# Two tokens instead of four interleaved in the one-hot tiles of the gate matrices

## The chip, the cores and the metric

The kernel runs on one core of one Trainium2 chip. The metric is the time of one execution on the device in microseconds (us); lower is better. TensorE multiplies matrices, VectorE (DVE in the profile) and ScalarE (ACT) do the elementwise work, and SyncE (SP) issues the loads of weights. SBUF is the memory on the chip that the engines read, PSUM the one into which TensorE writes.

## The reference, cut to what matters

A model of two blocks with two layers each runs over 256 tokens of width 1024. The change lies in the PEER layer of the first block, which runs twice (once a layer). Each of 8 heads of a token picks 16 of 128 x 128 experts by the sum of two scores, and the outputs are summed with a softmax over the 16 as the gate:

```python
def block(t):
    q = (t @ w_pq).reshape(T, PEER_HEADS, 2, PEER_HALF)
    s = jnp.einsum('thpk,hpnk->thpn', q, sub_keys)
    top_s, top_i = lax.top_k(s, PEER_TOPK)
    cand_s = top_s[:, :, 0, :, None] + top_s[:, :, 1, None, :]
    cand_i = top_i[:, :, 0, :, None] * N_KEYS + top_i[:, :, 1, None, :]
    best_s, best_pos = lax.top_k(cand_s.reshape(...), PEER_TOPK)
    experts = jnp.take_along_axis(cand_i.reshape(...), best_pos, axis=-1)
    gate = jax.nn.softmax(best_s, axis=-1)
    act = jax.nn.gelu(jnp.einsum('td,thkd->thk', t, expert_down[experts]))
    return jnp.einsum('thk,thkd->td', gate * act, expert_up[experts])
```

## The kernel before

The kernel doesn't gather experts. It computes the activation of every one of the 16384 experts for every token (the "down" loop), multiplies it with a gate that is zero nearly everywhere, and multiplies the result with the whole second table (the "up" loop). For a token the gates form a matrix of 128 x 128 (first index by second index): the product of a one-hot matrix of rows [128 pairs of head and place, 128] and a one-hot matrix of columns [128 pairs, 128] whose ones are replaced by the gates. The gate is held as two float16 parts, so each token takes two matmuls that add up in PSUM.

**The down loop.** `peer` (from line 932) runs 64 steps `jp` of two units. A unit is `mtile` (line 233): 24 matmuls of 256 columns in float32r (8 blocks times three products of high and low parts), on weights that `Stream` loads over SP and splits into two parts, the high one by ScalarE (line 95) and the low one by VectorE (line 100). Three pairs of tiles `whi`, `wlo` take turns, so the split runs about two units ahead. `gelu` (line 965) puts the activations of a step away, ScalarE alone or with a multiply on VectorE (line 975) for the tokens whose gates came first.

**The background.** `peer_select` (line 798) is a generator; `peer` takes steps of it between units by a budget: a unit adds 1400 (`BG`), each step subtracts the number that it yields. It first finds the experts, and after each block of 128 tokens transposes the four lists (first index, second index, low part and high part of the gate) so that the pairs lie on partitions, into the table `TT` (lines 886 to 889). Then it makes the gate matrices, four tokens (a group) at a time, 64 groups a layer; a group takes two steps of 800 (`GC`):

- line 924: `is_equal` of a counter `io4` with the first and second index, on VectorE: both one-hot matrices of four tokens, 1024 float16 a partition.
- lines 926 and 927: the group before the last is put away by `evac` (line 894): ScalarE writes the part of the activations that isn't there yet (line 901), VectorE multiplies into the part that is (line 904). The latter grows as the loop goes on.
- line 928: the one-hot columns times the two parts of the gate, one instruction of 1024 float16.
- lines 909 to 915: `gate_mm` of the group before, eight matmuls of 128 x 128 x 128 in float16 for four tokens.

The one-hot tiles lie in `w6`, two sets that take turns. In a set the four tokens are interleaved: `O` is [128 pairs, 3 kinds, 128 places, 4 tokens], and token t's matrix is read as `O[:, s, :, t]`, one element of 2 bytes in every 8 bytes, both as the weights and as the moving operand:

```python
self.mm(o, O[:, 0, :, t], O[:, 1, :, t], True, False)
self.mm(o, O[:, 0, :, t], O[:, 2, :, t], False, True)
```

All other operands of matmuls in the down loop are read element after element. The order of the instructions on each engine is that of the program.

Of the kernel before, what the change touches and what calls it, by code (L numbers as in the profile page):

```python
# [20 lines left out]
# columns of the per-channel vectors, [128, count] each  # L21
# [10 lines left out]
class Stream:  # L32
    """Loads run ahead in one queue, in the order of use; tiles of weights are split into two
    float32r parts a few units before they are needed."""
# [36 lines left out]
    def mark(self):  # L71
        """nothing behind this place is split before it is passed"""
        self.todo.append((None, None, None))
# [44 lines left out]
    def raw_due(self, ahead=0):  # L118
        """the next raw item was loaded in front of the tiles in use, or not far behind"""
        return self.raw_q and self.raw_q[0][2] < self.at + ahead  # L120


class Kern:
# [16 lines left out]
    def __init__(self, nc, tc, ctx, a, out):  # L140
# [22 lines left out]
        # parts that change to float32r where the experts come  # L163
# [24 lines left out]
    def reset(self, lo=20480):  # L188
        """scratch: parts of the arena that the loads leave alone"""
        self.scr_at = [[self.arena, lo, 25088 if self.late else 26624], [self.arena, 0, 4096]]  # L190
        if self.a3 is not None:
            self.scr_at.append([self.a3, 0, 6144])

    def second(self):
        """from here on other tiles of scratch serve, and the loads have eight places"""
        S = self.S
        self.late = True
        self.w6 = self.arena[:, 25088:].rearrange("p (a b) -> p a b", b=256)
        self.fr0 = self.rp.tile([128, 4096], F32R, name="fr0", tag="r0")
        self.fw6 = self.rp.tile([128, 1024], F32R, name="fw6", tag="w6")  # L200
        S.drop = self.r0s
        for s in self.r0s:
            if any(s is f for f in S.free):
                S.free.remove(s)
        self.reset()

    def rounded(self):
        """float32r tiles for the experts"""
        self.a3 = None
        self.fa3 = self.rp.tile([128, 6144], F32R, name="fa3", tag="a3")  # L210
# [22 lines left out]
    def mtile(self, o, h):  # L233
        """o[128 outputs, 256 tokens] from the next unit of weights and h (d on partitions)."""
        hi, lo = self.S.next()
        self.poll()
        for k in range(8):
            s = slice(k * 128, (k + 1) * 128)
            self.mm3(o, (hi[:, s], lo[:, s]), (h[0][:, k, :], h[1][:, k, :]), k == 0, k == 7)

    def mtile2(self, os, h, lead=None):
        """two tiles at once, as the blocks of h come"""
# [39 lines left out]
    def gemv(self, l, m, cb, pool=0):  # L282
        """columns m, m + 1 of layer l's modulation, from the next raw item, without their bias"""
# [32 lines left out]
    def sq_mm(self, sq, ss, col, cols=8):  # L316
        """column sums of sq [128, 256], tokens on partitions, into columns col, cols + col"""
        for tb in range(2):
            o = tb * cols + col
            self.mm(ss[:, o:o + 1], sq[:, tb * 128:(tb + 1) * 128], self.ones[:, 0:1], True, True)  # L320

    def sums(self):
        """opens the sums of squares of x, tokens on partitions"""
# [4 lines left out]
    def sum_mm(self, sq, ss, k):  # L328
        """adds block k's squares [128, 256]"""
# [11 lines left out]
    def warm(self, n):  # L341
        """keeps the tensor engine's clock up while it would wait"""
# [5 lines left out]
    def warm_root(self):  # L348
        """has the table of the square root loaded"""
        self.nc.scalar.activation(self.one, self.epst, AF.Sqrt)  # L350

    def root(self, parts, n, d):
        """1 / sqrt(mean + eps) for the sums over the last axis of parts [128, n, ...]"""
# [6 lines left out]
    def spread(self, r):  # L360
        """r: for both blocks of tokens a column -> [128, 256], the same on all partitions"""
# [5 lines left out]
    def rstd(self, ss, r=None):  # L367
        """for both blocks of tokens a column of 1 / rms"""
# [6 lines left out]
    def norm(self, r, g, sc, sh, keep=None):  # L375
        """hi, lo of x * rstd * g * (1 + sc) + sh"""
# [25 lines left out]
    def lead(self, cb):  # L402
        """the first norm, two blocks at a time as the columns of their scale and shift come"""
# [31 lines left out]
    def x_step(self, ps, k, g, ss):  # L435
        """block k of x and its squares, whose sums the caller takes later"""
# [5 lines left out]
    def out_open(self):  # L442
        """x += g * (w_out^T h) with the channels of h in any order: four banks stay open"""
# [4 lines left out]
    def out_step(self, h, k, g=None):  # L448
        """one block of 128 channels of h; with g it is the last"""
# [29 lines left out]
    def add_mixer1(self, l, ada, every):  # L479
        """ada: pairs of modulation columns, their loads between those of the weights"""  # L480
# [15 lines left out]
    def mixer1(self, l, h, g, lead=None):  # L496
# [7 lines left out]
        # q and k, channels on partitions; heads c and c + 4 share a tile  # L504
# [47 lines left out]
        # v and the gating half, tokens on partitions  # L552
# [10 lines left out]
        # normalised q, k  # L563
# [46 lines left out]
        # y holds the three branches: attention 0..3, convolution 4..5, gating 6..7  # L610
# [79 lines left out]
        # group norm of the gating half  # L690
# [62 lines left out]
    def act(self, jp):  # L753
        """two activations of every token"""
# [3 lines left out]
    def up_order(self, i):  # L758
        """pairs whose room goes to the loads come first"""
# [3 lines left out]
    def add_peer_up(self, l, extra):  # L763
        """extra: modulation columns (layer, m0, n) whose loads go between"""
# [11 lines left out]
    def top16(self, src, n, val, idx, tmp):  # L776
        """top 16 of each row of src [128, cnt, n]; a generator, one step per row pair"""
# [19 lines left out]
    def peer_select(self, qT, keys, st):  # L797
        """top experts of every token and head -> gates and indices with the pairs on partitions,
        then the gate matrix of every token, multiplied into the activations."""
# [18 lines left out]
        TT = self.sm.tile([128, 4, 256], F16, name="TT")  # L818
# [12 lines left out]
        for tb in range(2):  # L831
# [16 lines left out]
            # softmax over the 16 best, in two float16 parts of gate * 2^15  # L848
# [10 lines left out]
            # place among the candidates -> places in the two lists  # L859
# [29 lines left out]
            nc.scalar.copy(TT[:, :, tb * 128:(tb + 1) * 128], pt)  # L889
            yield 10  # L890
        # gate matrices
# [18 lines left out]
        def gate_mm(O, t0):  # L910
            ps = self.bank()
            for t in range(4):
                o = ps[:, t * 128:(t + 1) * 128]
                self.mm(o, O[:, 0, :, t], O[:, 1, :, t], True, False)
                self.mm(o, O[:, 0, :, t], O[:, 2, :, t], False, True)
            pend.append((ps, t0))

        for t0 in range(0, 256, 4):
            # one-hot rows and columns, the columns times the gate's parts
            o = t0 // 4 % 2 * 3  # L920
            O = self.w6[:, o:o + 3, :].bitcast(F16).rearrange("p s (j t) -> p s j t", t=4)
            io = self.io4[:, None, :, :].to_broadcast([128, 2, 128, 4])
            bc = lambda i: TT[:, i:i + 2, None, t0:t0 + 4].to_broadcast([128, 2, 128, 4])
            TX(O[:, 0::2], io, bc(0), op=OP.is_equal)
# [3 lines left out]
            TX(O[:, 1:3], O[:, 2:3].to_broadcast([128, 2, 128, 4]), bc(2), op=OP.mult)  # L928
            if last is not None:
                gate_mm(*last)  # L930
            last = (O, t0)
# [6 lines left out]
    def peer(self, l, h, g2, extra):  # L938
# [16 lines left out]
        # the arena is the activations' from here on  # L955
# [40 lines left out]
        # up: tokens stationary, the table moving  # L996
# [76 lines left out]
    def gla(self, h, g):  # L1073
# [16 lines left out]
        # decay  # L1090
# [22 lines left out]
        # values, tokens on partitions  # L1113
# [52 lines left out]
        def states(hd):  # L1166
            """the state after every chunk"""
# [96 lines left out]
    def softplus(self):  # L1264
        """8 softplus(-lambda) and its negative"""
# [23 lines left out]
    def lru(self, h, g):  # L1289
# [28 lines left out]
        def wgate(w, o, bn, b):  # L1318
            """a gate of half b, block-diagonal"""
# [141 lines left out]
    def route(self, h, hf, ht):  # L1461
        """combine weights, one-hot groups and ranks of the tokens inside their group"""
# [10 lines left out]
        # the tokens, rows  # L1473
# [23 lines left out]
        # top two of each group of four  # L1497
# [9 lines left out]
        # the first group with the largest sum  # L1507
# [8 lines left out]
        # tokens of the same group in front of each token; their count after the last  # L1516
# [6 lines left out]
        # rank inside the group, ties to the lower index  # L1523
# [35 lines left out]
    def experts(self, S, base, ht, w, oh, rk, g2, r, first=None, lent=()):  # L1559
        """slots base..base+127 of every group through the group's four experts"""  # L1560
# [19 lines left out]
        def gather(g2_):  # L1580
            """the tokens of two groups"""
# [46 lines left out]
        def turn(e):  # L1628
            """the hidden rows of expert e, channels on partitions"""
# [97 lines left out]
    def moe(self, l, h, hf, g2):  # L1727
# [22 lines left out]
        # groups of more than 128 tokens: their other slots  # L1750
# [14 lines left out]
def build(nc, tc, ctx, a, out, upto=99):  # L1765
# [7 lines left out]
    # modulation columns that load while the experts' second table does  # L1773
    extra = [[(0, 40, 8, "c"), (1, 0, 48, "c"), (2, 0, 24, "c2")], [(2, 24, 24, "c2"), (3, 0, 48, "c2")]]

    # the order of every load of the program
# [76 lines left out]
def _mtiles(w):  # L1853
    """[1024, N] -> [N / 256, 128, 2 * 1024]: two tiles of 128 outputs to a load."""
# [5 lines left out]
def arrays_of(inputs):  # L1860
# [39 lines left out]
    # modulation, [4 layers, 24, 128, 2 * 1024]  # L1900
    ada = np.stack([f["w_ada"][0], f["w_ada"][1], f["ada_w_2"][0], f["ada_w_2"][1]])
    A["ada"] = c(ada.transpose(0, 2, 1).reshape(4, 24, 2, 128, 1024).transpose(0, 1, 3, 2, 4).reshape(4, 24, 128, 2048))
    # attention bias by distance
# [72 lines left out]
```

## Time and profile before

| | us |
|---|---|
| median of 3 runs (2841.46 to 2842.47) | 2842.35 |
| span of the profiled execution | 2840.8 |
| TensorE busy in it | 2758.2 (97%) |
| VectorE busy | 2309.9 (81%) |
| ScalarE busy | 1566.3 (55%) |
| stage in which the gate matrices are made, layer 0 | 374.5 to 640.8 |
| the same, layer 1 | 1329.5 to 1595.9 |

The stages are taken from the first and last `is_equal` of line 924 in each layer. The busy time of TensorE counts a matmul from its issue to its modelled end, and neighbours overlap; how fast matmuls follow each other is read from their starts. On VectorE, too, the next instruction starts a little before the end of the one before.

### The profile page before, as it was taken

The numbers are of one execution on the slowest core, as the hardware profiler recorded it, in microseconds if no ns is written. First come the engines' busy times: TensorE is split into PE (matmuls) and PEld (weight loads), VectorE is DVE, ScalarE is ACT, GpSimd is POOL, SyncE is SP. The second block draws the span as 40 slices with busy tenths as digits, with TensorE's granted clock in tenths as the row PEclk, the third lists the DMA queues.
The fourth block names the chain that finished last, engine by engine and source line by source line (L and its number), as shares of the span: only waits on it lengthen the run. The fifth ranks groups of instructions, "written<-read, shape, count | busy, mean of one in ns | idle before, by whom it ended". The sixth has DMA issues, their size and how long they took to land. (4 is left out here: it accounts for less than half of the span.)

```text
span 2840.8 us, 43874 instructions
## 1 busy us (share of the span) xinstructions
PE 2758.2 (97%) x17371; PEld 2485.0 (87%) x17371; DVE 2309.9 (81%) x3701; ACT 1566.3 (55%) x2250; POOL 68.1 (2%) x60
## 2 busy tenths in 40 slices
PE   6899999999999999999999999999999999989998
PEld 5799999998888889999999888888888887978886
DVE  7858988896788866698789868887479997779997
ACT  4554454434544445455444454455567786767785
POOL 3400000000000000000000000000000000000000
PEclk9899999999999989999999999999999999999998
DMA  9461544445899943335444479986249998359894
GB/s 379 187 239 58 173 164 142 142 148 198 334 405 359 334 169 136 125 120 177 135 149 136 172 260 371 357 337 227 90 161 358 342 349 303 135 184 364 326 361 159
DMA packets 93751, 658.09 MB, mean 232 GB/s; under 512 B 10932, under 2 KB 12468, under 8 KB 14808
## 3 DMA queue, kind: packets, MB, share of 16 engines
q1 hardware_dynamic: 90432, 649.44, 62.0%
q10 hardware_dynamic: 3096, 5.68, 0.6%
q8 instruction: 140, 2.29, 0.3%
q14 instruction: 83, 0.68, 0.1%
HBM read 654.03 MB, written 1.05 MB: 231 GB/s over the span
## 5 line engine op out<-in xcount | busy, mean ns | idle before, releaser
L100 DVE TENSOR_TENSOR wlo<-arena,whi 128x1024 fp32r<-128x1024 f32 x610 | 734.6, 1221 | 229.3 <-ACT whi L95 216.7
L226 PE MATMUL bank<-hthi,whi 128*128 128x256 f32 x2920 | 851.4, 292 | 17.7 <-ACT whi L95 9.5
L95 ACT CAST whi<-arena 128x1024 fp32r<-128x1024 f32 x610 | 631.7, 1044 | 386.0 <-PE bank L226 375.6
L226 PE MATMUL bank<-htlo,whi 128*128 128x256 f32 x2920 | 834.9, 286 | 4.0 <-DVE htlo L386 2.5
L226 PE MATMUL bank<-hthi,wlo 128*128 128x256 f32 x2920 | 833.3, 285 | 4.8 <-DVE wlo L100 4.7
L95 ACT CAST whi<-r 128x1024 fp32r<-128x1024 f32 x331 | 347.8, 1051 | 527.3 <-PE bank L226 514.6
L226 PEld LDWEIGHTS bank<-hthi,whi 128*128 128x128 f32 x2920 | 566.3, 194 | 30.7 <-ACT whi L95 9.8
L226 PE MATMUL bank<-whi,hthi 128*128 128x512 f32 (+1 forms) x1472 | 573.3, 389 | 2.4 <-ACT hthi L265 2.4
L226 PEld LDWEIGHTS bank<-htlo,whi 128*128 128x128 f32 x2920 | 565.1, 194 | 10.2 <-DVE htlo L386 7.9
L226 PE MATMUL bank<-wlo,hthi 128*128 128x512 f32 (+1 forms) x1472 | 571.3, 388 | 0.5 <-DVE wlo L100 0.5
L226 PE MATMUL bank<-whi,htlo 128*128 128x512 f32 (+1 forms) x1472 | 571.5, 388 | 0.2
L226 PEld LDWEIGHTS bank<-hthi,wlo 128*128 128x128 f32 x2920 | 563.9, 193 | 6.3 <-DVE wlo L100 6.1
L100 DVE TENSOR_TENSOR wlo<-r,whi 128x1024 fp32r<-128x1024 f32 x331 | 404.9, 1225 | 152.9 <-ACT whi L95 150.9
L226 PEld LDWEIGHTS bank<-whi,hthi 128*128 128x128 f32 x1472 | 276.4, 188 | 58.4 <-ACT hthi L265 2.8
L226 PEld LDWEIGHTS bank<-whi,htlo 128*128 128x128 f32 x1472 | 276.3, 188 | 57.5 <-DVE htlo L266 1.1
L226 PEld LDWEIGHTS bank<-wlo,hthi 128*128 128x128 f32 x1472 | 276.4, 188 | 56.4 <-DVE wlo L100 1.2
L292 DVE SCALAR_TENSOR_TENSOR arena<-arena 128x1024 f32<-128x1024 f32 x136 | 163.6, 1240 | 0.0
L226 PE MATMUL bank<-w 128*128 128x128 f16 x1024 | 142.0, 296 | 1.3 <-DVE w L928 1.3
L226 PE MATMUL bank<-whi,fw 128*128 128x512 f32 x360 | 121.8, 392 | 1.7 <-ACT fw L265 1.5
L904 DVE SCALAR_TENSOR_TENSOR arena<-bank,arena 128x416 f32<-128x416 f32 (+23 forms) x128 | 123.3, 963 | 0.0
L100 DVE TENSOR_TENSOR fa<-arena,fa 128x1024 fp32r<-128x1024 f32 x96 | 117.5, 1224 | 5.2 <-ACT fa L95 0.3
L95 ACT CAST fa<-arena 128x1024 fp32r<-128x1024 f32 x96 | 101.0, 1052 | 27.0 <-PE bank L226 26.7
(341 smaller groups left out, 2815.3 us busy)
## 6 DMA issues: line engine op xcount, KB each, us to landing
r<-in_pdown SPq DMA_DIRECT2D x110, 1024.0 KB, 4.8
arena<-in_pup SPq DMA_DIRECT2D x81, 1024.0 KB, 6.6
arena<-in_ada SPq DMA_DIRECT2D x72, 1024.0 KB, 7.0
arena<-in_mg SPq DMA_DIRECT2D x64, 1024.0 KB, 5.8
arena<-in_mu SPq DMA_DIRECT2D x64, 1024.0 KB, 6.0
arena<-in_md SPq DMA_DIRECT2D x64, 1024.0 KB, 6.4
r<-in_pup SPq DMA_DIRECT2D x47, 1024.0 KB, 5.7
r<-in_ada SPq DMA_DIRECT2D x24, 1024.0 KB, 6.8
```

The source lines that it names most:

```text
L95: k.nc.scalar.copy(hi[:, :n], ap)
L100: self.k.nc.vector.tensor_sub(lo[:, :n], ap, hi[:, :n].bitcast(F32))
L226: self.nc.tensor.matmul(o, l, r, start=start, stop=stop)
L292: self.nc.vector.scalar_tensor_tensor(w, w, 1.0, cb, op0=OP.mult, op1=OP.mult, accum_out=o)
L904: nc.vector.scalar_tensor_tensor(o[:, :, :j - j0], p4[:, :, j0:j], 1.0 / GSC, o[:, :, :j - j0], op0=OP.mult, op1=OP.mult)
```

## The change

The set of one-hot tiles is ordered anew: two pairs of tokens (a = 0, 1), and in each pair the two tokens (b = 0, 1) interleaved. Token t = 2a + b is now read as one element of 2 bytes in every 4 bytes. An instruction of VectorE reads and writes runs of two float16 instead of four wherever an index or a gate is spread over the 128 places. `TT` holds, for each group of four tokens, its 16 numbers (four lists by four tokens) side by side, so that the operands still fit three dimensions; the copy of line 889 writes it in runs of four. The multiply becomes two instructions of 512 elements: first the low part into its own place, then the high part in place. `is_equal` stays one instruction of 1024. The number and size of the matmuls stay, as does the order of the steps and what they yield. The diff also removes comments and doc strings, which makes no instruction.

```diff
-        TT = self.sm.tile([128, 4, 256], F16, name="TT")
+        TT = self.sm.tile([128, 64, 16], F16, name="TT")
...
-            nc.scalar.copy(TT[:, :, tb * 128:(tb + 1) * 128], pt)
+            nc.scalar.copy(TT[:, tb * 32:(tb + 1) * 32, :].rearrange("p g (i t) -> p g i t", t=4),
+                           pt.rearrange("p i (g t) -> p g i t", t=4))
...
-        def gate_mm(O, t0):
+        def gate_mm(R, C, t0):
             ps = self.bank()
             for t in range(4):
+                a, b = divmod(t, 2)
                 o = ps[:, t * 128:(t + 1) * 128]
-                self.mm(o, O[:, 0, :, t], O[:, 1, :, t], True, False)
-                self.mm(o, O[:, 0, :, t], O[:, 2, :, t], False, True)
+                for n in range(2):
+                    self.mm(o, R[:, a, :, b], C[:, n, a, :, b], n == 0, n == 1)
             pend.append((ps, t0))
...
-            O = self.w6[:, o:o + 3, :].bitcast(F16).rearrange("p s (j t) -> p s j t", t=4)
-            io = self.io4[:, None, :, :].to_broadcast([128, 2, 128, 4])
-            bc = lambda i: TT[:, i:i + 2, None, t0:t0 + 4].to_broadcast([128, 2, 128, 4])
-            TX(O[:, 0::2], io, bc(0), op=OP.is_equal)
+            O = self.w6[:, o:o + 3, :].rearrange("p s b -> p (s b)").bitcast(F16)
+            R = O[:, 0:512].rearrange("p (a j t) -> p a j t", a=2, t=2)
+            C = O[:, 512:].rearrange("p (s a j t) -> p s a j t", s=2, a=2, t=2)
+            bc = lambda i, n: (TT[:, t0 // 4, 4 * i:4 * (i + n)].rearrange("p (c t) -> p c t", t=2)[:, :, None, :]
+                               .to_broadcast([128, 2 * n, 128, 2]))
+            TX(O[:, :1024].rearrange("p (c j t) -> p c j t", c=4, t=2),
+               self.io4[:, None, :, 0:2].to_broadcast([128, 4, 128, 2]), bc(0, 2), op=OP.is_equal)
             yield self.GC
             if len(pend) == 2:
                 evac(*pend.popleft())
-            TX(O[:, 1:3], O[:, 2:3].to_broadcast([128, 2, 128, 4]), bc(2), op=OP.mult)
+            for n in (1, 0):
+                TX(C[:, n], C[:, 0], bc(3 - n, 1), op=OP.mult)
             if last is not None:
                 gate_mm(*last)
-            last = (O, t0)
+            last = (R, C, t0)
             yield self.GC
```

## Rows read from the trace of the kernel before

**Rows 1.** Busy by stretch: length, PE, PEld, DVE, ACT, POOL, clock, DMA share, GB/s.

```profile
374.50:640.80 266.30, 266.30 (x2231) 262.92 (x2229) 227.48 (x309) 119.17 (x249) 0.00 (x0) 1.00 0.43 147
1329.50:1595.90 266.40, 266.40 (x2232) 263.00 (x2229) 227.50 (x309) 119.19 (x249) 0.00 (x0) 1.00 0.43 147
```

**Rows 2.** Timeline of TensorE, one group of gate matmuls: start, length, count.

```profile
603.06 0.28 PE L226 MATMUL bank<-hthi,wlo 128*128 128x256 f32 x1
603.18 1.11 PE L226 MATMUL bank<-w 128*128 128x128 f16 x8
604.04 0.37 PE L226 MATMUL bank<-hthi,whi 128*128 128x256 f32 x1
604.24 0.28 PE L226 MATMUL bank<-htlo,whi 128*128 128x256 f32 x1
```

**Rows 3.** The same view at the four transposes of line 888.

```profile
296.48 0.40 PE L888 MATMUL bank<-ident,a 128*128 128x128 f16 x4
296.71 0.33 PE L226 MATMUL bank<-arena 128*128 128x128 f32 x1
```

**Rows 4.** One tile's or line's instructions, float16 on TensorE: ns min/median/max.

```profile
L226 PEld LDWEIGHTS <-w x1024: 112/117/138, 380.3 to 1600.9; 128*128 128x128 f16 x171
L226 PE MATMUL bank<-w x1024: 283/297/301, 380.4 to 1601.0; 128*128 128x128 f16 x171
...
L888 PEld LDWEIGHTS <-a x16: 96/98/99, 296.5 to 1329.5; 128*128 128x128 f16 x16
L888 PE MATMUL bank<-ident,a x16: 219/219/230, 296.5 to 1329.5; 128*128 128x128 f16 x16
```

**Rows 5.** Timeline of TensorE in the up loop, float32r with 512 columns.

```profile
900.30 0.39 PE L226 MATMUL bank<-whi,htlo 128*128 128x512 f32 x1
900.52 0.39 PE L226 MATMUL bank<-whi,hthi 128*128 128x512 f32 x1
```

**Rows 6.** Groups of VectorE by line and shape: busy, mean ns of one, idle before.

```profile
L100 DVE TENSOR_TENSOR wlo<-r,whi 128x1024 fp32r<-128x1024 f32 x329 | 403.0, 1226 | 150.1 <-ACT whi L95 148.1
...
L924 DVE TENSOR_TENSOR w<-io,TT 128x1024 f16<-128x1024 f16 x128 | 88.1, 688 | 15.2 <-PE bank L226 14.6
...
L266 DVE TENSOR_TENSOR htlo<-arena,hthi 128x512 fp32r<-128x512 f32 x104 | 71.2, 686 | 4.3 <-ACT hthi L265 4.3
...
L881 DVE TENSOR_TENSOR a<-a 128x1024 f16<-128x1024 f16 x8 | 5.5, 692 | 0.3
...
L882 DVE TENSOR_TENSOR a<-a 128x512 f16<-128x512 f16 x8 | 3.4, 425 | 0.3
```

**Rows 7.** Timeline of VectorE, two neighbours of a group.

```profile
614.50 0.69 DVE L928 TENSOR_TENSOR w<-w,TT 128x1024 f16<-128x1024 f16 x1
615.11 0.69 DVE L924 TENSOR_TENSOR w<-io,TT 128x1024 f16<-128x1024 f16 x1
```

**Rows 8.** Busy times as in rows 1, cut at every eighth is_equal of layer 0.

```profile
374.50:407.30 32.80, 32.80 (x278) 32.42 (x276) 23.89 (x34) 16.62 (x30) 0.00 (x0) 1.00 0.49 163
407.30:440.80 33.50, 33.50 (x282) 33.06 (x282) 26.46 (x38) 16.02 (x35) 0.00 (x0) 1.00 0.44 154
440.80:475.40 34.60, 34.60 (x292) 34.17 (x291) 28.72 (x39) 16.40 (x37) 0.00 (x0) 1.00 0.42 141
475.40:509.20 33.80, 33.80 (x285) 33.36 (x284) 28.69 (x39) 15.36 (x35) 0.00 (x0) 1.00 0.41 137
509.20:542.40 33.20, 33.20 (x280) 32.77 (x279) 29.43 (x39) 14.41 (x33) 0.00 (x0) 1.00 0.45 153
542.40:576.30 33.90, 33.90 (x286) 33.46 (x285) 30.63 (x40) 14.31 (x31) 0.00 (x0) 1.00 0.38 130
576.30:611.10 34.80, 34.80 (x294) 34.37 (x293) 31.38 (x47) 14.40 (x28) 0.00 (x0) 1.00 0.44 152
611.10:640.80 29.70, 29.70 (x251) 29.32 (x250) 28.28 (x42) 11.63 (x25) 0.00 (x0) 1.00 0.42 143
```

**Rows 9.** Instructions on the table TT: ns min/median/max.

```profile
L889 ACT COPY TT<-bank x4: 586/586/586, 296.9 to 1329.8; 128x512 f16<-128x512 f16 x4
```

## The prediction

> **What bounds the kernel now.** I read four views, in this order. First the busy times by stretch: in the two stages in which the gate matrices are made, TensorE is busy for 266.30 of 266.30 us and 266.40 of 266.40 us at a granted clock of 1.00, VectorE for 227.5 us, ScalarE for 119 us [rows 1]. The reader is to see that nothing of these stages waits for VectorE, ScalarE or a load: a us off TensorE's stream is a us off the time until another engine takes over. The two stages are alike to 0.1 us, so one is worked out and doubled. Outside them the change touches four copies and the last two groups of each layer.
>
> Second, TensorE's timeline at one group [rows 2]. Here the starts matter, not the lengths, since matmuls overlap. The eight matmuls of the group last 1.11 us together, one of them 0.297 [rows 4], so the seven steps between them take (1.11 - 0.297) / 7 = 0.116 us each. The whole group, from its first matmul at 603.18 to the second float32r matmul behind it at 604.24, takes 1.06 us; less one float32r step of 0.12 (603.06 to 603.18) that is 0.94 us a group, of which 7 x 0.116 = 0.81 are the steps and 0.13 the last matmul.
>
> Third, the same view where float16 is read element by element: the four transposes, with 128 columns as well, last 0.40 us together, one of them 0.219 [rows 3, 4], which makes a step of (0.40 - 0.219) / 3 = 0.060 us. So the gate matmuls step at half the pace of matmuls of the same type and size. What differs is the distance of the elements, 8 bytes in place of 2.
>
> Fourth, VectorE by shape and in its own timeline, and the stage cut in eight [rows 6 to 8], to see how much room it leaves as the gates proceed.
>
> **The change part by part.** *The matmuls' operands, 8 bytes apart before, 4 bytes after.* No row of the trace has float16 at a distance of 4 bytes. [...] The transposes have the same type and count, packed: 0.060. [...] The other end is 0.116, no gain. I take 0.060, as type, size and loading of weights are those of the transposes, and keep 0.067 and 0.116 for the range. The weights aren't what paces the group: their load takes 117 ns against 98 ns packed [rows 4], 19 ns more, while the step is 56 ns longer, and packed loads of 98 ns go with steps of 60.
>
> The last matmul of a group stays at 0.12: behind it stands a float32r matmul that is 0.37 long in place of 0.28 [rows 2], as its weights come late, and that is not changed. A group then takes 7 x 0.060 + 0.12 = 0.54 us, 0.40 less than 0.94.
>
> [...]
>
> *VectorE.* `is_equal` keeps its 1024 elements in runs of two instead of four. Runs of four cost nothing: 688 ns, against 692 ns for 1024 float16 in one run [rows 6]. So I put runs of two at 688 ns as well; the other end, one element per cycle, is a rival below. The multiply of 0.69 us becomes two of 512 elements, 425 ns each [rows 6]. On VectorE the next instruction starts before the end of the one before: 615.11 - 614.50 = 0.61 us for a length of 0.69 [rows 7], 0.08 less. Two halves occupy 2 x (0.425 - 0.08) = 0.69 us in place of 0.61, so a group costs VectorE 0.08 us more. If the second half waited for the first to end (as the sums in a chain of line 882 do: 0.3 us idle over eight, some 0.04 each) it were 0.345 + 0.04 + 0.08 more for the pair, in all 0.21. Below nothing there is no room: two instructions do the work of one on as many elements. I take 0.08, by the rows of an unwaited neighbour, since the two halves write different places.
>
> *The copy into TT.* Four of 586 ns in the program [rows 9]. Writing in runs of four may lengthen it; twice as long would be 2.3 us in all, on ScalarE, which is idle for over half of each stage [rows 1], and nobody on TensorE waits for it. I cost it at nothing; without that cover it is 2.3 us at most.
>
> *What is late next.* Faster groups ask the same loads in less time: 147 GB/s over a stage [rows 1] become about 160, and the first of the eight windows has run at 163 with TensorE busy throughout [rows 8]. VectorE is the one that is late next. Its room in the eight windows is length less busy time [rows 8]: 8.91, 7.04, 5.88, 5.11, 3.77, 3.27, 3.42 and 1.42 us. It shrinks since the part of the activations that line 904 multiplies grows. The change takes 0.08 x 8 = 0.64 us of each (0.56 in the last, with seven `is_equal`), which leaves 8.27, 6.40, 5.24, 4.47, 3.13, 2.63, 2.78 and 0.86. TensorE offers 0.40 x 8 = 3.2 us a window (2.8 in the first and last, with seven groups of matmuls). The smaller of the two counts: 2.8 + 3.2 + 3.2 + 3.2 + 3.13 + 2.63 + 2.78 + 0.86 = 21.8 us a stage, of 24.8 offered. The two groups that remain behind each stage are made while VectorE is in arrears; I give them nothing.
>
> **The sum.** 2 x 21.8 = 43.6 us. The profiled span of 2840.8 becomes 2797.2; the median of the runs is 1.55 us over that span, and I keep this: 2842.35 - 43.6 = 2798.8, say 2799 us. Its own bounds: with all eight matmuls of a group at 0.056 to 0.060 (gain 0.49) and no growth on VectorE, the windows give 3.4 + 3 x 3.9 + 3.77 + 3.27 + 3.42 + 1.42 = 27 us a stage, 2788; with steps of 0.067 (gain 0.94 - 0.60 = 0.34) and 0.21 on VectorE, 2.4 + 3 x 2.7 + 2.09 + 1.59 + 1.74 - 0.05 = 15.9, 2811.
>
> **The rivals.** *Half the way.* The step falls only to the middle of 0.060 and 0.116, 0.088, because reads of 4 bytes apart collide more than packed ones, or weights are then the slower side. The gain is 0.94 - (7 x 0.088 + 0.13) = 0.19 us a group; the windows give 1.3 + 6 x 1.5 + 0.86 = 11.3 us a stage, 2820. For it: the weights' load is also longer now. [...]
>
> *Any gap halves the pace.* [...] TensorE's stream stays, and the 0.08 on VectorE lies in the room of every window, even the last (0.86 left): 2842, no change. For it: the trace has no float16 with gaps but this one. [...]
>
> *VectorE falls to one element per cycle, slower.* [...] Then `is_equal` takes 1226 ns (1024 elements at one a cycle), 0.54 more, and each half multiply 686 ns [rows 6], 2 x (0.686 - 0.08) - 0.61 = 0.60 more for the pair: 1.14 us a group. This decides from the point where the added time exceeds the room of a group, which is 1.11 us in the first window and 0.2 in the last [rows 8]: at once. The windows lose 0.2 + 2.1 + 3.2 + 4.0 + 5.4 + 5.9 + 5.7 + 6.6 = 33 us a stage, whatever TensorE does: 2842 + 66 = 2908. Against it: runs of four show no loss at all, not even a little. [...]
>
> **How the numbers follow.** Forecast 2799: 0.78. Half the way, 2820: 0.06. No gain, 2842: 0.09. Slower, 2908: 0.07. The range from 2786 to 2828 holds the first two with their bounds and a little on either side, 0.82 in all, and leaves out the others. About 0.2% (5.7 us) is what a measurement of this kernel can tell from no change; by that faster has 0.84, same 0.09, slower 0.07.
>
> **What would show it.** Right: the group of eight float16 matmuls lasts about 7 x 0.060 + 0.22 = 0.64 us in place of 1.11 and one of them about 0.22; the stages shorten from 266 to about 244 us; line 924 stays at 0.69 us, and the multiply shows as 256 instructions of 0.42; VectorE is busy for nearly all of the last windows, with TensorE now waiting there for `wlo` or the one-hot tiles, and little before the fifth. Wrong: matmuls that stay near 0.297 (no gain from 4 bytes); `is_equal` near 1.2 us; or a stage that shortens by less than its matmuls do already in the first four windows, which would mean a wait that I have not seen.

## The result and the profile after

| | us |
|---|---|
| before, median of 4 runs (2841.46 to 2842.47) | 2842.39 |
| after, median of 4 runs (2803.25 to 2807.64) | 2806.15 |
| ratio, with its 95% interval | 0.9874 (0.9862 to 0.9886) |
| forecast | 2799 (2786 to 2828) |

The change is faster by 36.2 us; 43.6 were forecast. The profiled execution has a span of 2801.5 us, 39.3 less than the one of before. Some 2.8 us of that lie outside the two PEER layers (the start alone happened to be 2 us shorter), so in what follows the layers are compared by themselves, from the last transpose of line 888 to the first matmul of the up loop with 512 columns: 278.7 us in both layers before, 261.0 and 260.0 after. These 36.4 us agree with the 36.2 between the medians.

First the instructions on the one-hot tiles (ns min/median/max), which answer to [rows 4] and [rows 6]:

```profile
L226 PEld LDWEIGHTS <-w x1024: 96/97/145, 378.5 to 1559.8; 128*128 128x128 f16 x171
L226 PE MATMUL bank<-w x1024: 217/218/308, 378.5 to 1559.8; 128*128 128x128 f16 x171
L934 DVE TENSOR_TENSOR w<-w,TT x256: 403/424/453, 375.6 to 1558.9; 128x512 f16<-128x512 f16 x128
...
L928 DVE TENSOR_TENSOR w<-io,TT x128: 681/684/693, 372.6 to 1555.0; 128x1024 f16<-128x1024 f16 x128
```

One matmul takes 218 ns in place of 297, which is what a transpose of packed float16 takes (219). `is_equal`, now line 928, keeps its pace (684 ns for runs of two, 688 for runs of four), and each half multiply (line 934) takes the 424 ns of a dense operation of that size.

The timeline of TensorE at one group, as in [rows 2]:

```profile
481.81 0.63 PE L226 MATMUL bank<-w 128*128 128x128 f16 x8
482.25 0.36 PE L226 MATMUL bank<-hthi,whi 128*128 128x256 f32 x1
482.45 0.28 PE L226 MATMUL bank<-htlo,whi 128*128 128x256 f32 x1
...
602.04 0.62 PE L226 MATMUL bank<-w 128*128 128x128 f16 x8 [0.70 <-DVE w L934]
...
623.52 1.04 PE L226 MATMUL bank<-w 128*128 128x128 f16 x8 [3.17 <-DVE w L934]
```

The eight last 0.63 us in place of 1.11, a step of (0.63 - 0.218) / 7 = 0.059. The group, counted as before, takes 482.45 - 481.81 - 0.12 = 0.52 us in place of 0.94: 0.42 saved, 27 us over the 64 groups of a layer. The last two rows show the other side: late in the stage TensorE stands and waits for the multiply, 0.70 us here, and 3.17 us behind the stage, before the last group. All that TensorE waits for in layer 0 from the first `is_equal` to the up loop, before (where line 928 is the multiply) and after (line 934), in us, times and the longest:

```profile
PE bank L226 <- DVE w L928: 0.6, 1, 0.6
...
PE bank L226 <- DVE w L934: 6.2, 7, 3.2
```

The last group takes 1.04 us in place of 0.63, and the float32r matmuls behind it step by 0.21 us in place of 0.12:

```profile
624.68 0.41 PE L226 MATMUL bank<-htlo,whi 128*128 128x256 f32 x1
624.89 0.41 PE L226 MATMUL bank<-hthi,wlo 128*128 128x256 f32 x1
```

This is TensorE's clock. The stretch from the last `is_equal` to the up loop by busy times (the third number from the right is the granted clock), in layer 0 before, and in both layers after:

```profile
640.80:653.20 12.40, 10.55 (x88) 9.99 (x86) 11.54 (x17) 4.77 (x11) 0.00 (x0) 1.00 0.31 101
...
619.10:633.60 14.50, 10.12 (x71) 9.70 (x69) 11.46 (x18) 4.04 (x8) 0.00 (x0) 0.76 0.25 87
1555.00:1568.50 13.50, 9.17 (x71) 8.74 (x69) 11.46 (x18) 4.01 (x8) 0.00 (x0) 0.87 0.28 92
```

From 623.5 to 628.0 the granted clock is 0.50. An estimate from the steps: some twenty matmuls 0.09 us longer each, and the group and the step behind it 0.6 us longer, make 2.4 us in layer 0; sixteen longer matmuls make 1.5 us in layer 1. Without them the stretch would be 12.0 us in both layers.

The stage cut at every eighth `is_equal`, to be held against [rows 8] (length, then busy PE, PEld, DVE, ACT, POOL, clock, DMA share, GB/s):

```profile
372.60:402.40 29.80, 29.80 (x278) 29.50 (x276) 24.91 (x42) 16.11 (x29) 0.00 (x0) 1.00 0.54 179
402.40:432.50 30.10, 30.10 (x283) 29.76 (x282) 27.46 (x46) 15.98 (x34) 0.00 (x0) 1.00 0.49 173
432.50:464.20 31.70, 31.70 (x295) 31.36 (x295) 29.61 (x48) 16.88 (x38) 0.00 (x0) 1.00 0.45 150
464.20:495.00 30.80, 30.80 (x288) 30.46 (x288) 29.35 (x47) 15.35 (x35) 0.00 (x0) 1.00 0.44 155
495.00:525.80 30.80, 30.80 (x291) 30.41 (x291) 30.05 (x47) 14.60 (x34) 0.00 (x0) 1.00 0.50 167
525.80:557.30 31.50, 31.50 (x292) 31.10 (x290) 31.23 (x48) 15.31 (x33) 0.00 (x0) 1.00 0.41 138
557.30:589.70 32.40, 31.05 (x286) 30.24 (x286) 32.13 (x54) 13.72 (x27) 0.00 (x0) 1.00 0.47 163
589.70:619.10 29.40, 27.61 (x252) 26.62 (x251) 29.16 (x48) 11.57 (x24) 0.00 (x0) 1.00 0.42 144
```

The windows are shorter by 3.0, 3.4, 2.9, 3.0, 2.4, 2.4, 2.4 and 0.3 us, 19.8 in all (21.8 forecast). The reader is to see the handover: in the first six windows TensorE is busy throughout, and VectorE's room falls from 4.9 us to 0.3; in the last two VectorE is busy for all but 0.25 us and TensorE is not. The windows are cut at instructions of VectorE, so what a window is shorter by isn't what TensorE gains in it: the fifth holds 291 matmuls where that of before held 280 [rows 8], since VectorE falls behind the loop. Counted by its matmuls (0.12 us for one of float32r, 0.52 for a group), TensorE loses nothing in the first six windows and 1.9 and 2.5 us in the last two.

Last, VectorE's timeline around the pair of multiplies, which answers to [rows 7]:

```profile
617.09 1.12 DVE L905 SCALAR_TENSOR_TENSOR arena<-bank,arena 128x416 f32<-128x416 f32 x1
618.13 0.29 DVE L905 SCALAR_TENSOR_TENSOR a<-bank,a 128x72 f32<-128x72 f32 x1
618.33 0.88 DVE L934 TENSOR_TENSOR w<-w,TT 128x512 f16<-128x512 f16 x2
619.12 0.68 DVE L928 TENSOR_TENSOR w<-io,TT 128x1024 f16<-128x1024 f16 x1
```

From the start of the pair to the next instruction it is 0.79 us; the one multiply of before had 0.61. A group costs VectorE 0.18 us more, not 0.08.

### The profile page after: what moved, and what is told of

Same layout as the page of the kernel before. It is cut to its first block, busy times and chain, and to the rows that moved or that the text cites. A ratio compares the mean times of both kernels' runs of the same rounds, so it can differ in the third digit from the quotient of the medians.

```text
span 2801.5 us, 44002 instructions
## 1 busy us (share of the span) xinstructions
PE 2706.1 (97%) x17371; PEld 2431.3 (87%) x17371; DVE 2321.0 (83%) x3829; ACT 1565.3 (56%) x2250; POOL 63.6 (2%) x60
## 5 line engine op out<-in xcount | busy, mean ns | idle before, releaser
L95 ACT CAST fa<-arena 128x1024 fp32r<-128x1024 f32 x96 | 101.0, 1052 | 27.0 <-PE bank L226 26.7
L934 DVE TENSOR_TENSOR w<-w,TT 128x512 f16<-128x512 f16 x256 | 108.1, 422 | 4.4
```

The costliest lines, as they stand in the source:

```text
L95: k.nc.scalar.copy(hi[:, :n], ap)
L934: TX(C[:, n], C[:, 0], bc(3 - n, 1), op=OP.mult)
```

## The experiments

All times are medians; each set of kernels was timed beside runs of the kernel before on the same chip, whose median stands beside them, so kernels of different sets are compared by the ratio or by "a layer", the stretch defined above (mean of the two in the profiled execution).

| kernel | us | before beside it | ratio (95%) | a layer |
|---|---|---|---|---|
| after | 2806.15 | 2842.39 | 0.9874 (0.9862 to 0.9886) | 260.5 |
| e1, distances set by group | 2846.11 (one run) | 2842.42 | | 281.4 |
| e2, two multiplies in the kernel before | 2843.07 | 2842.42 | 1.0004 (0.9994 to 1.0013) | 278.9 |
| e3, low half left out | 2791.34 | 2842.42 | 0.9820 (0.9804 to 0.9836) | 252.0 |
| e4, low half moved between | 2801.29 | 2842.42 | 0.9854 (0.9837 to 0.9870) | 258.2 |
| e5, packed | 2916.96 (one run) | 2840.11 | | 316.9 |
| e6, graded pace | 2790.69 | 2840.11 | 0.9816 (0.9801 to 0.9831) | 252.2 |
| e7, all groups sooner | 2805.16 | 2840.11 | 0.9877 (0.9861 to 0.9892) | 260.7 |
| e8, e4 and e6 together | 2787.26 | 2840.11 | 0.9811 (0.9797 to 0.9824) | 251.7 |
| e9, graded pace in the kernel before | 2841.42 | 2841.97 | 0.9998 (0.9989 to 1.0008) | 278.6 |

**e1: what the distance costs, and on which operand.** The places that the matmuls read are set by group, in 30 pairs of distances (the two pairs at the end only fill the round of 32):

```diff
+    PAIRS = [(w, m) for w in (1, 2, 3, 4, 8) for m in (1, 2, 3, 4, 6, 8)] + [(2, 2), (4, 4)]
...
+                dw, dm = self.PAIRS[t0 // 4 % 32]
+                W, M = R[:, 0:128 * dw], R[:, 0:128 * dm]
+                if dw > 1:
+                    W = W.rearrange("p (j d) -> p j d", d=dw)[:, :, t % dw]
+                if dm > 1:
+                    M = M.rearrange("p (j d) -> p j d", d=dm)[:, :, (t + 1) % dm]
                 for n in range(2):
-                    self.mm(o, R[:, a, :, b], C[:, n, a, :, b], n == 0, n == 1)
+                    self.mm(o, W, M, n == 0, n == 1)
...
-            last = (R, C, t0)
+            last = (O, C, t0)
```

> The changed kernel, except that the eight matmuls of a group read their two operands at distances that the group sets: weights every 1, 2, 3, 4 or 8 elements of float16 (2 to 16 bytes), moving operand every 1, 2, 3, 4, 6 or 8, in all 30 pairs, in turn. The places read aren't those of the tokens, so the gate matrices are left undefined; number, size and order of all instructions stay. My theory: the moving operand alone sets the step, at about 0.056 us for 2 and 4 bytes and 0.117 for 8 and more, as if one read of 8 bytes served one matmul column in each of two cycles; 6 bytes in between (0.07 to 0.09). The weights' distance changes the step by less than 0.01 up to 8 bytes. Rival one: the weights set the step (0.117 wherever weights are 8 bytes apart, whatever the moving operand). [...]

TensorE's timeline, groups in the order of time. The first five have the weights 4 bytes apart and the moving operand 4, 6, 8, 12 and 16; the last two have the moving operand 4 bytes apart and the weights 8 and 16:

```profile
408.10 0.63 PE L227 MATMUL bank<-w 128*128 128x128 f16 x8
411.50 0.86 PE L227 MATMUL bank<-w 128*128 128x128 f16 x8
415.10 1.09 PE L227 MATMUL bank<-w 128*128 128x128 f16 x8
418.90 1.54 PE L227 MATMUL bank<-w 128*128 128x128 f16 x8
423.16 2.00 PE L227 MATMUL bank<-w 128*128 128x128 f16 x8
...
460.22 0.67 PE L227 MATMUL bank<-w 128*128 128x128 f16 x8
483.58 0.72 PE L227 MATMUL bank<-w 128*128 128x128 f16 x8
```

The moving operand decides. Over all 30 pairs the median step from start to start is 0.056 to 0.062 us with it packed, 0.057 to 0.064 at 4 bytes, 0.087 to 0.092 at 6, 0.115 to 0.124 at 8, 0.171 to 0.179 at 12 and 0.227 to 0.235 at 16. The spread within each is the weights' distance, which costs 0.004 us at most up to 8 bytes and 0.005 to 0.009 at 16. The median hides the first step of a group, which grows with it (0.114 us with the weights 16 bytes apart, 0.067 packed, the moving operand packed in both). So rival one falls. My own picture falls too in its second half: I had the cost level off at 8 bytes (0.117 for 16), and it doubles again; the read of 8 bytes in it was a guess, which no trace shows. From 4 bytes on the step grows in proportion to the distance, 0.014 us for each byte (weights packed); below that the distance hardly counts, 0.056 us packed and 0.058 at 4 bytes. So 6 bytes are not free: they cost half as much again as 4, and 8 bytes twice as much.

**e2: the split alone.** In the kernel before:

```diff
-            TX(O[:, 1:3], O[:, 2:3].to_broadcast([128, 2, 128, 4]), bc(2), op=OP.mult)
+            for s in (1, 2):
+                TX(O[:, s], O[:, 2], TT[:, s + 1, None, t0:t0 + 4].to_broadcast([128, 128, 4]), op=OP.mult)
```

> The kernel before with one part of the change alone: the multiply of line 928 in two instructions of 512 elements, the second in place; tokens stay interleaved by four. In the changed kernel the pair takes 0.80 us from its start to the next instruction, 0.19 more than the one of before. My theory: at the old pace of the matmuls VectorE's room hides that in all but the last of the eight windows (1.42 us of room, 1.5 used): 2842 to 2845 us. Rival: the split costs by itself what the change brought less than forecast, 7 us: 2849 us or more.

2843.07 against 2842.42 us, no difference that the interval can tell. The last window, by its busy times:

```profile
609.90:639.70 29.80, 29.80 (x252) 29.43 (x251) 29.41 (x49) 11.74 (x24) 0.00 (x0) 1.00 0.40 142
```

TensorE is still busy throughout, while VectorE's room has gone from 1.42 us [rows 8] to 0.39. The split costs nothing as long as TensorE is slow; it eats the room that the faster matmuls need.

**e3: VectorE relieved.** The changed kernel without the multiply of the low part:

```diff
-            for n in (1, 0):
+            for n in (0,):
                 TX(C[:, n], C[:, 0], bc(3 - n, 1), op=OP.mult)
...
-                    self.mm(o, R[:, a, :, b], C[:, n, a, :, b], n == 0, n == 1)
+                    self.mm(o, R[:, a, :, b], C[:, 0, a, :, b], n == 0, n == 1)
```

> The changed kernel without the multiply of the low part of the gate: the second matmul of each token reads the high part again, so the gates come out wrong; the matmuls stay as many. It takes about 0.44 us a group off VectorE (0.80 for the pair becomes 0.35). My theory: the part of the matmuls' gain that was lost (27 us a layer offered, 18 kept) was lost to VectorE, so nearly all comes back: 2842 - 54 = 2788, at most 2792 us. Rival: the rest is lost elsewhere on TensorE, at the passage between float16 and float32r matmuls: 2802 to 2806 us.

2791.34 us, and a layer takes 252.0: 26.7 us less than before, nearly all of the 27 that the matmuls offer. In the last window TensorE is busy throughout again, at a length of 26.7 us:

```profile
588.20:614.90 26.70, 26.70 (x251) 26.40 (x250) 26.30 (x41) 11.58 (x24) 0.00 (x0) 1.00 0.46 159
```

So what the changed kernel does not keep is lost to VectorE, by TensorE's waits for it and by the clock that fell behind the longest of them: here that wait is 0.96 us, and the granted clock stays at 1.00 up to the up loop. The passage between float16 and float32r costs nothing more.

**e4: the wait between the halves.** The low half goes between the two parts of `evac`, where there are two:

```diff
+            low = lambda: TX(C[:, 1], C[:, 0], bc(2, 1), op=OP.mult)
             if len(pend) == 2:
-                evac(*pend.popleft())
-            for n in (1, 0):
-                TX(C[:, n], C[:, 0], bc(3 - n, 1), op=OP.mult)
+                evac(*pend.popleft(), low)
+            else:
+                low()
+            TX(C[:, 0], C[:, 0], bc(3, 1), op=OP.mult)
```

(`evac` now calls its last argument, `low`, behind its first multiply.)

> The changed kernel with the low half multiplied ahead of the second part of the putting away (line 904's instruction for the last 24 of the 128 places) where there is one, so that the second half no longer follows the first at once; same instructions otherwise. My theory: the second half waits some 0.12 us for the first to end since it overwrites what the first reads; in the last two of eight windows, the ones with the second part, this wait goes: 16 groups of 0.12 us, 2 us a layer, 2802 us. Rival: the wait is only passed on to the instruction between: 2806 us.

VectorE's timeline in the last window:

```profile
596.01 0.45 DVE L934 TENSOR_TENSOR w<-w,TT 128x512 f16<-128x512 f16 x1
596.35 0.27 DVE L905 SCALAR_TENSOR_TENSOR a<-bank,a 128x48 f32<-128x48 f32 x1
596.50 0.45 DVE L939 TENSOR_TENSOR w<-w,TT 128x512 f16<-128x512 f16 x1
596.84 0.71 DVE L931 TENSOR_TENSOR w<-io,TT 128x1024 f16<-128x1024 f16 x1
```

Each half now has 0.34 us to the next instruction, 0.68 for both in place of 0.79: the wait is worth 0.11 us a group, and it isn't passed on. In the changed kernel's trace the second half of all 128 pairs waits for a semaphore that VectorE itself raises, and starts 0.034 us behind the end of the first (median). A layer takes 258.2 us, 2.3 less than the changed kernel's mean and 1.9 less than its second layer, in which the clock fell for about as long as it does here (granted 0.87 behind the stage in both). The median is 2801.29 us, 2802 were expected; the ratio's interval still overlaps the changed kernel's, so it is the traces that show the gain.

**e5: no interleaving.** The one-hot tiles packed, each token by itself:

```diff
-            R = O[:, 0:512].rearrange("p (a j t) -> p a j t", a=2, t=2)
-            C = O[:, 512:].rearrange("p (s a j t) -> p s a j t", s=2, a=2, t=2)
+            R = O[:, 0:512].rearrange("p (a j t) -> p a j t", a=4, t=1)
+            C = O[:, 512:].rearrange("p (s a j t) -> p s a j t", s=2, a=4, t=1)
...
-            TX(O[:, :1024].rearrange("p (c j t) -> p c j t", c=4, t=2),
-               self.io4[:, None, :, 0:2].to_broadcast([128, 4, 128, 2]), bc(0, 2), op=OP.is_equal)
+            TX(O[:, :1024].rearrange("p (c j) -> p c j", c=8),
+               self.io1[:, None, :].to_broadcast([128, 8, 128]), bc(0, 2), op=OP.is_equal)
...
```

> The changed kernel with no tokens interleaved at all: each token's 128 places lie side by side (2 bytes apart), the counter is a packed row, and the index or gate of a token is spread over all 128 places, so VectorE reads that operand as one element again and again. My theory: TensorE steps as after the change (0.056), but VectorE falls to one element a cycle: is_equal about 1.22 us in place of 0.68, each half multiply 0.69 in place of 0.42, 1.06 us a group more; VectorE then sets the stage alone, 54 us a layer longer: about 2910 us. [...]

The tile's instructions (ns min/median/max):

```profile
L227 PE MATMUL bank<-w x1024: 216/219/314, 379.0 to 1674.2; 128*128 128x128 f16 x171
L935 DVE TENSOR_TENSOR w<-w,TT x256: 671/691/726, 376.1 to 1672.7; 128x512 f16<-128x512 f16 x128
...
L929 DVE TENSOR_TENSOR w<-io,TT x128: 1215/1218/1222, 373.2 to 1668.0; 128x1024 f16<-128x1024 f16 x128
```

TensorE gains nothing over runs of two (219 ns against 218), and VectorE falls to about half its pace: 1218 in place of 684 ns, 691 in place of 424. It is the slow rival of the prediction, one step further on: 2916.96 us, 2908 by the rival's sum. What both texts call one element a cycle is the pace of float32 in [rows 6], 1226 ns for 1024 elements and 686 for 512.

**e6: the gates paced by VectorE's room.** In the changed kernel, both steps of a group:

```diff
-            yield self.GC
+            yield 580 + 1.65 * t0
```

> The changed kernel with another pace of the background: a step of the gate matrices counts 580 + 1.65 t0 in place of 800 (t0 the first token of the group, 0 to 252), so the first groups come faster and the last slower, and the stage as a whole ends about where it did. No instruction is added or taken away. My theory: VectorE is out of room only in the last windows and idle for some 12 us in the first five; spread evenly, its work fits beside TensorE's and the lost 9 us a layer come back but for 1 or 2: 2788 to 2792 us. Rival: the loss is not one of VectorE's throughput late in the stage: 2804 to 2808 us.

The first and the last two of the eight windows by busy times:

```profile
373.30:398.30 25.00, 24.25 (x230) 23.79 (x228) 22.56 (x40) 13.57 (x25) 0.00 (x0) 1.00 0.51 172
...
545.60:579.70 34.10, 34.10 (x316) 33.77 (x315) 33.47 (x53) 15.84 (x29) 0.00 (x0) 1.00 0.45 155
579.70:612.00 32.30, 32.30 (x301) 31.96 (x300) 32.06 (x51) 14.26 (x29) 0.00 (x0) 1.00 0.49 164
```

Early windows shrink to 25 us and late ones grow to 32 to 34, and TensorE is busy throughout the stage but for 0.75 us at the start; its longest wait is 0.8 us, and the granted clock is 1.00 up to the up loop. A layer takes 252.2 us, 26.5 less than before; 2790.69 us.

**e7: sooner, but not graded.**

```diff
-    GC = 800
+    GC = 720
```

> The changed kernel with every step of the gate matrices at 720 in place of 800, so that all groups come a tenth sooner and the last ones have units of the down loop behind them. My theory (VectorE's throughput in the later windows): more groups per unit only fill VectorE earlier; the wait before the last groups (3.2 us a layer) goes, the waits inside the stage grow by about as much: 2802 to 2808 us. Rival: the loss is only the wait at the end, where the last two groups have nothing to hide behind: 2799 to 2800 us.

```profile
513.10:543.80 30.70, 29.41 (x274) 28.12 (x273) 30.42 (x47) 14.68 (x35) 0.00 (x0) 1.00 0.46 163
543.80:574.40 30.60, 28.41 (x259) 26.80 (x258) 30.33 (x49) 12.78 (x28) 0.00 (x0) 1.00 0.41 141
574.40:602.30 27.90, 25.44 (x232) 24.03 (x230) 27.66 (x48) 10.43 (x22) 0.00 (x0) 1.00 0.34 116
```

The wait before the last group is down to 0.7 us, but in each of the last three windows (busy times again) VectorE is full and TensorE stands for 1.3 to 2.5 us. A layer takes 260.7 us, as in the changed kernel: 2805.16 us. So the loss isn't only the wait at the end: where groups come faster than VectorE can make them, TensorE waits in the stage instead.

**e8: both.** The edits of e4 and e6.

> The graded pace and the low half between the two parts of the putting away, together. My theory: with the graded pace VectorE has a little room everywhere, so the second edit adds at most 1 us: 2787 to 2791 us. Rival: both act on what is short, and add up to the whole of what the matmuls offer and more room: below 2786 us.

2787.26 us, within what was expected; a layer takes 251.7. What TensorE still waits for in layer 0, from the first `is_equal` to the up loop:

```profile
PE bank L226 <- DVE w L939: 0.8, 1, 0.8
```

The changed kernel waited 6.2 us there. This is the lowest median of all, 0.9811 (0.9797 to 0.9824) of the kernel before, 53 us less; a layer is 27.0 us shorter, the whole of what the shorter reads offer. By the ratio e6 (0.9816) and e8 can't be told apart; a layer differs by 0.5 us, as expected. In e6's profile the granted clock is also 0.50 from 627.3 to 630.7, just behind the layer, which in e8's it isn't; each is one execution.

**e9: the graded pace without the change.** The edit of e6 in the kernel before.

> The kernel before (tokens interleaved by four, one multiply) with the graded pace of e6 alone: a step of the gate matrices counts 580 + 1.65 t0 in place of 800. My theory: before the change TensorE's stream alone sets the stages and VectorE has room in every window, so the pace is worth nothing there: 2840 to 2844 us. Rival: the graded pace is a gain of its own, whatever the matmuls' step, and the 15 us that it brought on top of the change aren't the change's own lost gain: 2825 to 2832 us.

2841.42 against 2841.97 us, nothing. The pace is worth something only behind the change (13 us by the medians beside their own kernel before, 17 by the layers); e6 gives back the change's own gain.

## Why the prediction was right, and by how much it was off

The bound was read rightly: TensorE's stream set the stages, and the difference lies in the two layers.

The matmuls' term held. A step of 0.060 was forecast, 0.057 to 0.059 measured; a group saved 0.42 us, not 0.40, since its last matmul, which I had left at 0.12, shrank as well. The value taken, that of the packed transposes (0.060), was the right one. No run shows the 0.067 in the prediction's bounds; the runs show float32r, whose elements stand 4 bytes apart, at steps of 0.12 us for 256 columns and 0.22 for 512 [rows 2, 5], and 128 columns of float16 at 0.058 us with 4 bytes, 0.056 packed (e1). That the weights don't pace the group held too: their distance changed the median step by 0.009 us at most (e1).

The term that was mis-sized is VectorE's: 0.08 us a group forecast, 0.18 measured. The step that failed was "by the rows of an unwaited neighbour, since the two halves write different places". They do, but the second half writes over what the first reads, which is all that ties the two together, and it waits; e4 shows the wait at 0.11 us. The upper end of the bound, put at 0.21 (its own working, 0.08 + 0.04 + 0.08, gives 0.20), was the nearer one: the 0.04 idle of the chain of line 882 is what the second half shows (0.034). With 0.18, the sum over [rows 8] as the prediction made it gives 2.9 + 3 x 3.4 + 2.3 + 1.8 + 2.0 + 0.2 = 19.4 us, and 19.8 were measured. That these agree so well is in part luck, for the windows don't agree one by one: the third and fourth shrank by 2.9 and 3.0 in place of 3.4, the sixth and seventh by 2.4 in place of 1.8 and 2.0. "The smaller of the two counts" treats each window by itself; in the trace VectorE's arrears are carried on, and TensorE pays for them only from the seventh window on.

A second term was left out: I gave the two groups behind the stage nothing, and the stretch there grew from 12.4 to 14.5 us in layer 0 and 13.5 in layer 1. VectorE's arrears fall due there, as a wait of 3.17 us in place of 0.65, and behind it TensorE's granted clock fell to 0.50, which the prediction didn't think of. The fall costs some 2.4 and 1.5 us by the estimate above, which is all of that growth and more. In e3, e6, e7 and e8 that wait is under 1 us and the clock stays at 1.00 in this stretch; in e4 it is 2.8 us and the clock falls. No run separates the clock from the wait. 2 x 19.8 - 2.1 - 1.1 = 36.4.

The rivals: half the way and no gain fell with the first group of the trace. The slow one did not come, as runs of two keep VectorE's pace (684 ns for `is_equal`, 688 before); e5 shows that runs of one would have brought it, at about its price. What was rightly forecast of the picture after: VectorE full in the late windows, and TensorE waiting there, for the one-hot tiles, and not before.

What stays open: the price of distances over 16 bytes on the moving operand was not tried, nor was a second half multiply with a place of its own. Why the weights' distance costs so little is not shown, nor at what length of a wait the clock falls.

## What to carry to other kernels

The moving operand of a matmul was paid here by the bytes it spans, from 4 bytes a column on (128 columns of float16 in e1, weights packed): an interleave of two elements of 2 bytes was all but free (a step of 0.058 us, 0.056 packed), one of four halved the pace (0.115). Interleave no wider than VectorE needs to keep its pace, which here was a run of two (684 ns for 1024 elements, 1218 with none). When the bound engine gets faster, sum the next engine's room stretch by stretch, count the waits between its neighbours, and move paced background work to where that room is.

## What the runs showed of the hardware that was not expected

- The moving operand's step keeps growing with the distance of its elements: 0.058, 0.087, 0.115, 0.171 and 0.227 us for 128 float16 columns at 4, 6, 8, 12 and 16 bytes (e1, weights packed).
- The weights bear gaps far better: 16 bytes apart costs 0.005 to 0.009 us in the median step, and some 0.05 in the first step of a group, while the load itself grows from 98 to 146 ns (e1).
- The second half multiply, which overwrites what the first reads, started 0.034 us after the end of the first (after), where neighbours on VectorE that don't wait start 0.08 us ahead of it [rows 7]: 0.11 us a pair (e4).
- Behind a wait of 3.17 us (after) and of 2.81 us (e4) TensorE's granted clock fell from 1.00 to 0.50, and 256 columns of float32r stepped by 0.21 us in place of 0.12. Behind waits of 0.64 us (before) and 0.96 us (e3) in the same place it stayed at 1.00.
